# When columns that come back from DRAM are split, and how a memory's layer norm is laid out, in a two-layer hybrid decoder

## The chip, the core and the metric

The kernel runs on one core of one Trainium2 chip. A core has a matrix engine (PE; its weight loads are shown apart as PEld), a vector engine (DVE), a scalar engine (ACT), GpSimd (POOL) and a sync engine (SP). Each takes its own queue of instructions strictly in order, and they wait for each other by semaphores. SP and POOL also issue DMAs here, SP the loads of weights and constants, POOL the round trips through DRAM. Matrix products land in PSUM, which has eight banks per partition; all else lives in SBUF, 128 partitions wide.

The metric is the device time of one execution in microseconds. Lower is better. The median of three executions is the time of a version.

## What is computed

Two layers of a decoder over 256 positions with 1024 features, in float32. Each layer is a half-step SwiGLU block with its layer norm, three token mixers beside each other (a gated delta rule, a sliding-window attention, a cross-attention to a memory of 256 rows), a merge, a norm, and a second half-step SwiGLU block with its norm. Only these parts matter here:

```python
def swiglu(x, w_gu, w_down):
    gate, up = jnp.split(x @ w_gu, 2, axis=-1)       # D_FF = 2816
    return (jax.nn.silu(gate) * up) @ w_down

mem_n = layer_norm(mem, mem_ln_g, mem_ln_b)          # once, for both layers
for l in range(DEPTH):                               # DEPTH = 2
    x = layer_norm(ALPHA * x + 0.5 * swiglu(x, ffn1_gu[l], ffn1_down[l]), ...)
    ...
    k, v = jnp.split(mem_n @ w_mem_kv[l], 2, axis=-1)
    ...
    x = layer_norm(ALPHA * x + 0.5 * swiglu(x, ffn2_gu[l], ffn2_down[l]), ...)
```

`layer_norm` takes mean and variance over the 1024 features of a row, subtracts, multiplies by `rsqrt(var + 1e-5)`, scales by `g` and adds `b`.

## The kernel before

**Products in three passes.** Every float32 operand is split into a high part in a reduced format and the remainder (`split`, lines 115 to 117: a cast on ACT, then a subtraction on DVE), and a product is three matmuls: high by high, high by low, low by high (`mm3`). Weights come as one stream in the order of use, in units of 128 x 1024 words, 512 KB each. `unit` loads a unit on SP into `raw` (three buffers) and splits it into `whi` and `wlo` (five buffers each). So each unit costs ACT one cast and DVE one subtraction.

**The feed-forward block** (class `Ffn`, four times in the program). The 2816 hidden columns are worked in eleven groups of 256. For a group, PE computes gate and up for both halves of the positions, four units and 48 matmuls, into two PSUM banks of the pool `acc`, which has four. So two groups are in flight. `out` (lines 332 to 348) then does, for each half `tb`, a SiLU on ACT from PSUM to the tile `t` (line 338) and the product by `up` on DVE (line 339), which is the last reader of the half's bank. It follows a 32x32 block transpose on DVE (line 341), four stores on POOL to a DRAM tile `tr` (line 345) and one load on POOL back to SBUF (line 346), so that the hidden columns lie on partitions. The result is split again into a tile `u` (line 348): `u<-t` on ACT, `u<-t,u` on DVE. All of `t`, its transpose and the loaded columns share the tag `t2` with four buffers. After the eleven groups, `projA` multiplies the 22 `u` tiles by the down weights, 22 units, into banks for four outputs (`full_rows`: four banks of `acc` and one of `at`).

**What sets the order.** A planner lays out each engine's queue. It goes by priorities: what is traced earlier goes first among what it takes as ready; a unit's load and split are given a place 300 instructions earlier than where they are traced. Two marks bind it: `load` keeps a DMA on SP behind everything that was traced on SP before, and `issue_after(ins)` queues what a block traces on the engine of `ins`, and only on that engine, behind `ins`. The order is fixed when the program is built; on the chip an engine that waits for one instruction waits with all that stand behind it.

**The memory.** During the first feed-forward block of layer 0, `rest` calls small pieces of other work after given groups (the table `mid`; key `f` belongs to group `f // 2`). `memory_T` (lines 407 to 430) gives them: after f = 11 the two vectors `g` and `b` are loaded as broadcast rows of 512 KB each (`gb`), after 13 and 15 one half of the memory rows each is loaded into a tile `pp`, normed with `layernorm` (with the rsqrt done by integer start and three Newton steps, line 277) and turned by eight PE transposes into a PSUM tile `sm`, which is split into the tiles `mT` (`w0` to `w3`). After 16, `keep` stores these four tiles to DRAM, and layer 1 loads them again (`again`). `memory_kv` uses them right after the block.

Of the kernel before, what the change touches and what calls it, by code (L numbers as in the profile page):

```python
# [17 lines left out]
P = 128  # L18
# [19 lines left out]
@with_exitstack  # L38
def tile_trunk(ctx, tc, x, xT, mem, wst, lnp, memln, cvw, rows, cst, out):
    nc = tc.nc  # L40
# [55 lines left out]

    pos = [0]

    def unit(w=U, dst=None, cuts=1, behind=None):
        ahead = tc.high_priority(offset=AHEAD) if pos[0] >= 8 * P * U else nullcontext()  # L100
        raw = T(praw, [P, U], "raw")
        src = wst[pos[0]:pos[0] + P * w].rearrange("(p w) -> p w", p=P)
        pos[0] += P * w
        (ph, th), (pl, tl) = dst or ((phi, "whi"), (plo, "wlo"))
        with ahead:
            hi = T(ph, [P, U], th, F32R)
            lo = T(pl, [P, U], tl, F32R)
            for i in range(cuts):
                c = slice(i * w // cuts, (i + 1) * w // cuts)
                nc.sync.dma_start(raw[:, c], src[:, c])  # L110
                with tc.issue_after(behind) if behind else nullcontext():
                    split(hi[:, c], lo[:, c], raw[:, c])
        return hi, lo
# [58 lines left out]

    def projA(xt, w, kpu, nk, outs, tail=0, dsts=(), lead=0, after=None, behind=None, held=(), led=None):

# [26 lines left out]
        for uu in range(lead, nu - tail):  # L201
            for tb in range(2):
                run([uu], tb, range(len(outs[tb])))
        for uu in range(nu - tail, nu):
            get(uu)
# [47 lines left out]
    def layernorm(y, gB, bB, eps, src=None, fin=None, sizes=(512, 512)):  # L253
        n = min(sizes)
        st = T(p3, [P, 4, 6], "bnst")[:, :D // n, :]
        done = at_ = 0
        for j, size in enumerate(sizes):
            if src:
                src(j, slice(at_, at_ + size))
            at_ += size  # L260
            while done < at_:
                nc.vector.bn_stats(st[:, done // n, :], y[:, done:done + n])  # L262
                done += n
        mv = T(p3, [P, 2], "bnmv")
        nc.vector.bn_aggr(mv, st)  # L265
        rs = T(p3, [P, 1], "rstd")
        rt = T(p3, [P, 1], "rst")

        if src:
            nc.scalar.activation(rs, mv[:, 1:2], AF.Sqrt, bias=epsc[:, eps:eps + 1])  # L270
            nc.vector.reciprocal(rs, rs)
            nc.vector.scalar_tensor_tensor(rt, mv[:, 1:2], epsc[:, eps:eps + 1], rs, op0=ALU.add, op1=ALU.mult)
            nc.vector.scalar_tensor_tensor(rt, rt, -0.5, rs, op0=ALU.mult, op1=ALU.mult)
            nc.vector.scalar_tensor_tensor(rs, rt, 1.5, rs, op0=ALU.add, op1=ALU.mult)  # L274
        else:
            nc.vector.tensor_scalar(mv[:, 1:2], mv[:, 1:2], LN_EPS, None, ALU.add)
            rsqrt(rs, mv[:, 1:2], rt)
        for c in range(2):
            cc = slice(c * 512, (c + 1) * 512)
            nc.vector.scalar_tensor_tensor(y[:, cc], y[:, cc], mv[:, 0:1], gB[:, cc], op0=ALU.subtract, op1=ALU.mult)  # L280
            ins = nc.vector.scalar_tensor_tensor(y[:, cc], y[:, cc], rs, bB[:, cc], op0=ALU.mult, op1=ALU.add)  # L281
            if fin:
                fin(c)
        return ins.ins
# [9 lines left out]
    class Ffn:  # L294
        def __init__(self, before=None):
            self.units = []
            for q in range(KD // 2):
                if before:
                    before(q)
                self.units.append(unit(cuts=2 if before and q == 0 else 1))  # L300
            self.hu, self.bank = {}, {}

# [29 lines left out]
        def out(self, i, banks):  # L332
# [3 lines left out]
            for tb in range(2):  # L336
                g, u = (banks[tb][:, c:c + S].rearrange("p (j x) -> p j x", j=8) for c in (0, S))
                nc.scalar.activation(t[:, :, tb, :], g, AF.Silu)  # L338
                nc.vector.tensor_tensor(t[:, :, tb, :], t[:, :, tb, :], u, op=ALU.mult)  # L339
            z = T(p2, [P, 512], "t2", bufs=4)  # L340
# [5 lines left out]
            nc.gpsimd.dma_start(y, d.rearrange("b c q x -> (b c) (q x)"))  # L346
            hi, lo = (self.h(i)[:, n].rearrange("p a (t q s) -> p (a t) q s", t=2, q=4) for n in range(2))
            split(hi, lo, y.rearrange("p (q n s) -> p n q s", q=4, n=4))

        def rest(self, hT, tail, dsts, post, mid={}, behind=None):  # L350
            for i in range(1, NFT // 2):
# [9 lines left out]
                for f in (2 * i, 2 * i + 1):  # L361
                    if f in mid:
                        mid[f]()
            outs = full_rows()
            projA((lambda k: self.hu[k // 2][:, 0, k % 2, :], lambda k: self.hu[k // 2][:, 1, k % 2, :]), D, 1, NFT, outs, tail, dsts, after=post)

# [40 lines left out]
    def memory_T(mT, l):  # L407
# [13 lines left out]
        def vecs():  # L421
            got["gb"] = gb(memln[0], memln[1])
            mT.extend(T(pu, [P, 4, S], f"w{i}", F32R) for i in range(4))

        def rows_(tb):
            m = T(p2, [P, D], "pp")
            load(m, mem[tb * P:(tb + 1) * P, :])
            layernorm(m, *got["gb"], 0, None, lambda q: to_T(lambda q: (mT[q], mT[2 + q]), tb, m, q))

        return {13: again} if l else {11: vecs, 13: lambda: rows_(0), 15: lambda: rows_(1), 16: keep}  # L430

# [672 lines left out]
```

## Time and profile before

| | |
|---|---|
| median of 3 executions | 1369.0 us (1361.87 to 1371.48) |
| the profiled execution's own time | 1370.57 us |
| its span, first to last instruction | 1368.8 us |
| mean granted clock of PE | 0.977 of full speed |
| DMA, mean over the span | 192 GB/s |
| longest kinds of wait on ACT and DVE for the columns | ACT `u` for the load of `t` from `tr`: 130.9 us in 38 waits; DVE `u` for ACT `u`: 112.7 us in 45 |

A row of the profile's groups reads: line, engine, operation, what it writes `<-` what it reads, shapes, count | busy us in all, mean ns of one | idle us of the engine just before them, and what ended most of it. A row of the timeline starts with its time and its duration in us, and has in brackets how long the engine was idle before it and what it waited for. A row of stretches has the stretch, its length, the busy time of PE, PEld, DVE, ACT and POOL with the number of instructions, the granted clock of PE (1.00 is full), the DMA engines' busy share and GB/s. A row of waits has the total in us, the number and the longest.

### The profile page before, as it was taken

To read this page: it belongs to the slowest core of one execution; us is meant where nothing else is said; L and a number is where in the kernel's file an instruction comes from. 1 tells how busy PE (TensorE), PEld (TensorE's weight loads), DVE (VectorE), ACT (ScalarE), POOL (GpSimd) and SP (SyncE) were. 2 spreads that over 40 slices of the span, in tenths; PEclk is the share of its full clock that TensorE was granted. 3 is DMA by queue.
4 is the path that set the end of the run, shared out by engine and by line. 5 is a ranking of instruction groups with operands and counts; after the bars stand their busy time and mean duration, and the time that the engine had idled before them with its cause. 6 is when DMAs were issued, how large, how long until landed. Compare 5 with 4: busy or idle time off the path is not lost. (4 is left out here: it accounts for less than half of the span.)

```text
span 1368.8 us, 19252 instructions
## 1 busy us (share of the span) xinstructions
PE 1290.0 (94%) x7176; PEld 1099.4 (80%) x7176; DVE 850.7 (62%) x1270; ACT 652.6 (48%) x973; POOL 197.1 (14%) x355
## 2 busy tenths in 40 slices
PE   8979899999999999978999978999999999999797
PEld 6857789999878788766888757899987787887586
DVE  5576457796647865553675554668867388555445
ACT  6544343666665443443354343446657554444341
POOL 0222100002310012220011220000033100122200
PEclk9999999999999999998999998999999999999899
DMA  8878674755535647665677666656554355666663
GB/s 267 288 234 269 192 225 137 216 170 139 165 108 163 222 151 233 205 203 180 228 232 229 211 200 189 215 152 205 169 156 139 93 187 183 210 214 208 201 185 120
DMA packets 77726, 263.26 MB, mean 192 GB/s; under 512 B 11680, under 2 KB 12832, under 8 KB 77632
## 3 DMA queue, kind: packets, MB, share of 16 engines
q1 hardware_dynamic: 66176, 232.53, 52.9%
q0 software_dynamic: 11456, 29.51, 7.8%
q8 instruction: 56, 0.92, 0.3%
q14 instruction: 38, 0.31, 0.1%
HBM read 247.18 MB, written 14.81 MB: 191 GB/s over the span
## 5 line engine op out<-in xcount | busy, mean ns | idle before, releaser
L117 DVE TENSOR_TENSOR wlo<-raw,whi 128x1024 fp32r<-128x1024 f32 (+2 forms) x403 | 479.7, 1205 | 326.6 <-ACT whi L116 324.9
L116 ACT CAST whi<-raw 128x1024 fp32r<-128x1024 f32 (+2 forms) x403 | 410.0, 1034 | 441.4 <-DMA raw<-in_wst_dram 219.7
L126 PE MATMUL acc<-whi,hT 128*128 128x512 f32 (+1 forms) x1824 | 571.2, 389 | 25.1 <-DVE t L339 20.3
L126 PEld LDWEIGHTS acc<-whi,hT 128*128 128x128 f32 x1824 | 342.9, 189 | 99.9 <-DVE t L339 26.6
L126 PE MATMUL acc<-wlo,hT 128*128 128x512 f32 (+1 forms) x912 | 352.5, 387 | 0.3 <-DVE wlo L117 0.3
L126 PE MATMUL acc<-whi,u 128*128 128x512 f32 (+1 forms) x800 | 257.5, 386 | 30.8 <-DVE t L339 30.8
L126 PEld LDWEIGHTS acc<-whi,u 128*128 128x128 f32 x800 | 156.1, 197 | 63.0 <-DVE t L339 35.4
L126 PEld LDWEIGHTS acc<-wlo,hT 128*128 128x128 f32 x912 | 172.8, 189 | 33.2 <-DVE wlo L117 1.2
L345 POOL DMA_DIRECT2D tr<-t x176 | 96.1, 553 | 414.6 <-DVE t L341 407.7
L126 PE MATMUL acc<-wlo,u 128*128 128x512 f32 (+1 forms) x400 | 153.1, 383 | 0.0
L126 PE MATMUL acc<-hT,whi 128*128 128x256 f32 x672 | 122.3, 284 | 0.0
L126 PEld LDWEIGHTS acc<-hT,whi 128*128 128x128 f32 x672 | 104.7, 192 | 0.0
L117 DVE TENSOR_TENSOR u<-t,u 128x512 fp32r<-128x512 f32 x44 | 30.4, 691 | 104.6 <-ACT u L116 104.5
L126 PE MATMUL acc<-hT,wlo 128*128 128x256 f32 x336 | 95.0, 283 | 0.0
L116 ACT CAST u<-t 128x512 fp32r<-128x512 f32 x44 | 27.2, 619 | 130.9 <-DMA t<-tr 130.9
L126 PEld LDWEIGHTS acc<-wlo,u 128*128 128x128 f32 x400 | 78.8, 197 | 13.0
L126 PEld LDWEIGHTS acc<-hT,wlo 128*128 128x128 f32 x336 | 64.4, 192 | 0.0
L346 POOL DMA_DIRECT2D t<-tr x44 | 25.0, 568 | 184.9 <-DMA tr<-t 139.6
L126 PE MATMUL at<-whi,u 128*128 128x256 f32 x152 | 41.0, 294 | 0.0
L339 DVE TENSOR_TENSOR t<-t,acc 128x256 f32<-128x256 f32 x88 | 35.9, 414 | 3.5 <-ACT t L338 3.3
L473 DVE SCALAR_TENSOR_TENSOR t<-acc,cw,t 128x255 f32<-128x255 f32 (+2 forms) x72 | 34.4, 478 | 0.9
L338 ACT ACTIVATE t<-acc 128x256 f32<-128x256 f32 x88 | 32.6, 378 | 3.0 <-PE acc L126 3.0
(244 smaller groups left out, 1267.7 us busy)
## 6 DMA issues: line engine op xcount, KB each, us to landing
raw<-in_wst_dram SPq DMA_DIRECT2D x409, 512.0 KB, 4.3
tr<-t POOLq DMA_DIRECT2D x176, 64.0 KB, 3.7
t<-tr POOLq DMA_DIRECT2D x44, 256.0 KB, 3.2
raw<-in_wst_dram SPq DMA_DIRECT2D x16, 324.0 KB, 3.1
gB<-in_lnp_dram SPq DMA_DIRECT2D x6, 512.0 KB, 6.6
bB<-in_lnp_dram SPq DMA_DIRECT2D x6, 512.0 KB, 6.2
mdr<-w POOLq DMA_DIRECT2D x4, 512.0 KB, 6.0
w<-dr POOLq DMA_DIRECT2D x4, 512.0 KB, 10.4
```

The lines of the kernel that those rows point to most:

```text
L116: nc.scalar.copy(hi, src)
L117: return nc.vector.tensor_tensor(lo, src, hi.bitcast(F32), op=ALU.subtract).ins
L126: return pe(nc.tensor.matmul(*a, **k))
L338: nc.scalar.activation(t[:, :, tb, :], g, AF.Silu)
L339: nc.vector.tensor_tensor(t[:, :, tb, :], t[:, :, tb, :], u, op=ALU.mult)
L345: nc.gpsimd.dma_start(d[:, :, q].rearrange("b c x -> c b x"), z[32 * q:32 * q + 32].rearrange("c (b x) -> c b x", b=4))
L346: nc.gpsimd.dma_start(y, d.rearrange("b c q x -> (b c) (q x)"))
L473: nc.vector.scalar_tensor_tensor(yc[:, j, d:], b[:, j, :S - d], w[:, t:t + 1], yc[:, j, d:], op0=ALU.mult, op1=ALU.add)
```

## The change

Two things are changed. The split of the columns that come back from DRAM moves from the end of `out` to a new `settle`. It is called in the next group's `out`, behind the products of line 339, and for the last group in `projA`, behind the ninth unit of the down weights. The DVE half is queued behind the instruction given; the ACT half is only traced later. The small pieces of `mid` are queued, on DVE, behind the group's last product.

The memory's norm no longer turns rows into columns on PE. The host gives a second, feature-major copy of the memory (`memT`), and `mem_ln_g`, `mem_ln_b` by partitions. The row-major copy is read for the statistics only. Mean and reciprocal deviation of the 256 rows go through DRAM (512 words out, a broadcast of 2 KB to all 128 partitions back), and each half of the feature-major copy has the mean subtracted and the factor multiplied on DVE, is scaled and shifted on ACT with four instructions of 256 columns, and is split. The steps now stand at f = 8 (loads), 10 (statistics), 13 (load of the halves), 15, 17 (the halves) and 19 (`keep`).

```diff
@@ -94,7 +94,7 @@
         nc.scalar.copy(t.rearrange("p v k -> p (v k)"), zero.to_broadcast([P, 2 * S]))
 
 
-    pos = [0]
+    pos, newest = [0], [None]
 
     def unit(w=U, dst=None, cuts=1, behind=None):
         ahead = tc.high_priority(offset=AHEAD) if pos[0] >= 8 * P * U else nullcontext()
@@ -109,7 +109,7 @@
                 c = slice(i * w // cuts, (i + 1) * w // cuts)
                 nc.sync.dma_start(raw[:, c], src[:, c])
                 with tc.issue_after(behind) if behind else nullcontext():
-                    split(hi[:, c], lo[:, c], raw[:, c])
+                    newest[0] = split(hi[:, c], lo[:, c], raw[:, c])
         return hi, lo
 
     def split(hi, lo, src):
@@ -170,7 +170,7 @@
             (b,) = yield from projB_parts(xt, 2, 4)
             use(i, b)
 
-    def projA(xt, w, kpu, nk, outs, tail=0, dsts=(), lead=0, after=None, behind=None, held=(), led=None):
+    def projA(xt, w, kpu, nk, outs, tail=0, dsts=(), lead=0, after=None, behind=None, held=(), led=None, along=None):
 
         def one(k, kk, hi, lo, tb, j):
             ts = slice(tb * P, (tb + 1) * P)
@@ -201,6 +201,8 @@
         for uu in range(lead, nu - tail):
             for tb in range(2):
                 run([uu], tb, range(len(outs[tb])))
+            if along and uu == 8:
+                along(newest[0])
         for uu in range(nu - tail, nu):
             get(uu)
         turns = ()
@@ -266,15 +268,11 @@
         rs = T(p3, [P, 1], "rstd")
         rt = T(p3, [P, 1], "rst")
 
-        if src:
-            nc.scalar.activation(rs, mv[:, 1:2], AF.Sqrt, bias=epsc[:, eps:eps + 1])
-            nc.vector.reciprocal(rs, rs)
-            nc.vector.scalar_tensor_tensor(rt, mv[:, 1:2], epsc[:, eps:eps + 1], rs, op0=ALU.add, op1=ALU.mult)
-            nc.vector.scalar_tensor_tensor(rt, rt, -0.5, rs, op0=ALU.mult, op1=ALU.mult)
-            nc.vector.scalar_tensor_tensor(rs, rt, 1.5, rs, op0=ALU.add, op1=ALU.mult)
-        else:
-            nc.vector.tensor_scalar(mv[:, 1:2], mv[:, 1:2], LN_EPS, None, ALU.add)
-            rsqrt(rs, mv[:, 1:2], rt)
+        nc.scalar.activation(rs, mv[:, 1:2], AF.Sqrt, bias=epsc[:, eps:eps + 1])
+        nc.vector.reciprocal(rs, rs)
+        nc.vector.scalar_tensor_tensor(rt, mv[:, 1:2], epsc[:, eps:eps + 1], rs, op0=ALU.add, op1=ALU.mult)
+        nc.vector.scalar_tensor_tensor(rt, rt, -0.5, rs, op0=ALU.mult, op1=ALU.mult)
+        nc.vector.scalar_tensor_tensor(rs, rt, 1.5, rs, op0=ALU.add, op1=ALU.mult)
         for c in range(2):
             cc = slice(c * 512, (c + 1) * 512)
             nc.vector.scalar_tensor_tensor(y[:, cc], y[:, cc], mv[:, 0:1], gB[:, cc], op0=ALU.subtract, op1=ALU.mult)
@@ -298,7 +296,7 @@
                 if before:
                     before(q)
                 self.units.append(unit(cuts=2 if before and q == 0 else 1))
-            self.hu, self.bank = {}, {}
+            self.hu, self.bank, self.due = {}, {}, None
 
         def h(self, i):
             if i not in self.hu:
@@ -336,7 +334,8 @@
             for tb in range(2):
                 g, u = (banks[tb][:, c:c + S].rearrange("p (j x) -> p j x", j=8) for c in (0, S))
                 nc.scalar.activation(t[:, :, tb, :], g, AF.Silu)
-                nc.vector.tensor_tensor(t[:, :, tb, :], t[:, :, tb, :], u, op=ALU.mult)
+                ins = nc.vector.tensor_tensor(t[:, :, tb, :], t[:, :, tb, :], u, op=ALU.mult).ins
+            self.settle(ins)
             z = T(p2, [P, 512], "t2", bufs=4)
             nc.vector.transpose(z, t.rearrange("p j t x -> p (j t x)"))
             y = T(p2, [P, 512], "t2", bufs=4)
@@ -344,8 +343,16 @@
             for q in range(4):
                 nc.gpsimd.dma_start(d[:, :, q].rearrange("b c x -> c b x"), z[32 * q:32 * q + 32].rearrange("c (b x) -> c b x", b=4))
             nc.gpsimd.dma_start(y, d.rearrange("b c q x -> (b c) (q x)"))
-            hi, lo = (self.h(i)[:, n].rearrange("p a (t q s) -> p (a t) q s", t=2, q=4) for n in range(2))
-            split(hi, lo, y.rearrange("p (q n s) -> p n q s", q=4, n=4))
+            self.due = (i, y)
+
+        def settle(self, behind):
+
+            if self.due:
+                (i, y), self.due = self.due, None
+                hi, lo = (self.h(i)[:, n].rearrange("p a (t q s) -> p (a t) q s", t=2, q=4) for n in range(2))
+                with tc.issue_after(behind):
+                    split(hi, lo, y.rearrange("p (q n s) -> p n q s", q=4, n=4))
+            self.last = behind
 
         def rest(self, hT, tail, dsts, post, mid={}, behind=None):
             for i in range(1, NFT // 2):
@@ -360,9 +367,10 @@
                 self.out(i, banks)
                 for f in (2 * i, 2 * i + 1):
                     if f in mid:
-                        mid[f]()
+                        with tc.issue_after(self.last):
+                            mid[f]()
             outs = full_rows()
-            projA((lambda k: self.hu[k // 2][:, 0, k % 2, :], lambda k: self.hu[k // 2][:, 1, k % 2, :]), D, 1, NFT, outs, tail, dsts, after=post)
+            projA((lambda k: self.hu[k // 2][:, 0, k % 2, :], lambda k: self.hu[k // 2][:, 1, k % 2, :]), D, 1, NFT, outs, tail, dsts, after=post, along=self.settle)
 
     class Post:
 
@@ -419,15 +427,46 @@
                 nc.gpsimd.dma_start(mdr[i], flat(t.bitcast(F32)))
 
         def vecs():
-            got["gb"] = gb(memln[0], memln[1])
+            got["st"] = T(pu, [P, 2, 2], "mst")
+            got["gb"] = T(pu, [P, 2, KD], "mgb")
+            load(got["gb"], memln)
             mT.extend(T(pu, [P, 4, S], f"w{i}", F32R) for i in range(4))
-
-        def rows_(tb):
-            m = T(p2, [P, D], "pp")
-            load(m, mem[tb * P:(tb + 1) * P, :])
-            layernorm(m, *got["gb"], 0, None, lambda q: to_T(lambda q: (mT[q], mT[2 + q]), tb, m, q))
-
-        return {13: again} if l else {11: vecs, 13: lambda: rows_(0), 15: lambda: rows_(1), 16: keep}
+            got["m"] = [T(p2, [P, D], "pp") for _ in range(2)]
+            for tb in range(2):
+                load(got["m"][tb], mem[tb * P:(tb + 1) * P, :])
+
+        def rows_():
+
+            for tb in range(2):
+                mv = T(p3, [P, 2], "bnmv")
+                st = T(p3, [P, 4, 6], "bnst")[:, :2, :]
+                for j in range(2):
+                    nc.vector.bn_stats(st[:, j, :], got["m"][tb][:, j * 512:j * 512 + 512])
+                nc.vector.bn_aggr(mv, st)
+                nc.vector.tensor_copy(got["st"][:, 0, tb:tb + 1], mv[:, 0:1])
+                nc.vector.tensor_scalar(mv[:, 1:2], mv[:, 1:2], LN_EPS, None, ALU.add)
+                rsqrt(got["st"][:, 1, tb:tb + 1], mv[:, 1:2], T(p3, [P, 1], "rst"))
+            d = T(pd, [2, 2, P], "ms")
+            nc.gpsimd.dma_start(d.rearrange("a t p -> p a t"), got["st"])
+            got["row"] = T(pu, [P, D], "gB")[:, 0:512]
+            nc.gpsimd.dma_start(got["row"], d.rearrange("a t p -> (a t p)").partition_broadcast(P))
+
+        def halves_():
+            got["m"] = [T(p2, [P, 4, S], "pp") for _ in range(2)]
+            for q in range(2):
+                load(got["m"][q], memT_[:, q])
+
+        def half(q):
+            m = got["m"][q]
+            mean, rs = (got["row"][:, c:c + S].unsqueeze(1).to_broadcast([P, 4, S]) for c in (0, S))
+            nc.vector.tensor_tensor(m, m, mean, op=ALU.subtract)
+            nc.vector.tensor_tensor(m, m, rs, op=ALU.mult)
+            for j in range(4):
+                g, b = (got["gb"][:, n, 4 * q + j:4 * q + j + 1] for n in range(2))
+                nc.scalar.activation(m[:, j], m[:, j], AF.Identity, bias=b, scale=g)
+            split(mT[q], mT[2 + q], m)
+
+        return {13: again} if l else {8: vecs, 10: rows_, 13: halves_, 15: lambda: half(0), 17: lambda: half(1), 19: keep}
 
     def memory_kv(mT, behind):
         mx = (lambda k: mT[k // 4][:, k % 4, :], lambda k: mT[2 + k // 4][:, k % 4, :])
@@ -1083,9 +1122,10 @@
         "x": i["x"][0],
         "xT": np.ascontiguousarray(i["x"][0].T),
         "mem": i["mem"][0],
+        "memT": np.ascontiguousarray(i["mem"][0].T.reshape(2, 4, P, S).transpose(2, 0, 1, 3)),
         "wst": _stream(i),
         "lnp": np.stack([i["ln_g"], i["ln_b"]], 2),
-        "memln": np.stack([i["mem_ln_g"], i["mem_ln_b"]]),
+        "memln": np.ascontiguousarray(np.stack([i["mem_ln_g"], i["mem_ln_b"]]).reshape(2, KD, P).transpose(2, 0, 1)),
         "cvw": np.ascontiguousarray(i["dn_conv_w"].reshape(NL, 4, 12, P).transpose(3, 0, 2, 1)),
         "rows": np.concatenate([i["swa_sinks"], i["dn_a_log"], i["dn_dt_bias"], i["dn_norm_w"]], 1),
         "cst": _consts(),
```

More of the change, by code (lines that the diff above doesn't have):

```diff
@@ L38, in tile_trunk @@
 @with_exitstack
-def tile_trunk(ctx, tc, x, xT, mem, wst, lnp, memln, cvw, rows, cst, out):
+def tile_trunk(ctx, tc, x, xT, mem, memT_, wst, lnp, memln, cvw, rows, cst, out):
     nc = tc.nc
```

## The prediction, made before the changed kernel ran

> **What bounds the kernel now.** I read the page first, then the table of waits of PE, then the timelines of ACT, DVE, POOL and PE through one period of the second feed-forward block of layer 0, and last tables of busy time over chosen stretches.
>
> ```profile
> span 1368.8 us, 19252 instructions
> PE 1290.0 (94%) x7176; PEld 1099.4 (80%) x7176; DVE 850.7 (62%) x1270; ACT 652.6 (48%) x973; POOL 197.1 (14%) x355
> L126 PE MATMUL acc<-whi,hT 128*128 128x512 f32 (+1 forms) x1824 | 571.2, 389 | 25.1 <-DVE t L339 20.3 <-ACT whi L116 4.8
> L126 PE MATMUL acc<-whi,u 128*128 128x512 f32 (+1 forms) x800 | 257.5, 386 | 30.8 <-DVE t L339 30.8
> L116 ACT CAST u<-t 128x512 fp32r<-128x512 f32 x44 | 27.2, 619 | 130.9 <-DMA t<-tr 130.9
> ...
> PE acc L126 <- DVE t L339: 51.1, 24, 6.2
> ...
> L129 PE MATMUL sm<-cs,pp 128*128 128x128 f32 x16 | 3.6, 387 | 9.7 <-DVE pp L281 7.9 <-issue 1.8
> ```
>
> PE is busy for 94% of the span, so what can be won is its idle time, 1368.8 - 1290.0 = 78.8 us, and whatever part of its busy time runs slowly. Of the idle time 51.1 us (24 waits) end with the product of line 339, which frees a PSUM bank: 20.3 us where a group of the gate/up product starts, 30.8 us where the four down projections start. Another 9.7 us lie ahead of the 16 transposes of the memory's norm (last row). Why is line 339 late, though it takes 0.41 us? The timelines say:
>
> ```profile
> 598.33 0.50 PE L126 MATMUL acc<-whi,hT 128*128 128x512 f32 x1 [1.15 <-DVE t L339]
> ...
> 587.92 0.37 ACT L338 ACTIVATE t<-acc 128x256 f32<-128x256 f32 x1
> 592.00 1.05 ACT L116 CAST whi<-raw 128x1024 fp32r<-128x1024 f32 x1 [3.71 <-DMA raw<-in_wst_dram]
> 596.60 0.62 ACT L116 CAST u<-t 128x512 fp32r<-128x512 f32 x1 [3.54 <-DMA t<-tr]
> 597.13 0.38 ACT L338 ACTIVATE t<-acc 128x256 f32<-128x256 f32 x1
> ...
> 608.95 0.62 ACT L116 CAST u<-t 128x512 fp32r<-128x512 f32 x1 [3.44 <-DMA t<-tr]
> 609.47 0.38 ACT L338 ACTIVATE t<-acc 128x256 f32<-128x256 f32 x1
> ...
> 597.25 0.69 DVE L117 TENSOR_TENSOR u<-t,u 128x512 fp32r<-128x512 f32 x1 [2.94 <-ACT u L116]
> 597.86 0.41 DVE L339 TENSOR_TENSOR t<-t,acc 128x256 f32<-128x256 f32 x1
> 598.31 0.71 DVE L341 STREAM_TRANSPOSE t<-t 128x512 f32<-128x512 f32 x1
> 609.60 0.69 DVE L117 TENSOR_TENSOR u<-t,u 128x512 fp32r<-128x512 f32 x1 [2.83 <-ACT u L116]
> 610.21 0.41 DVE L339 TENSOR_TENSOR t<-t,acc 128x256 f32<-128x256 f32 x1
> ...
> 599.32 2.17 POOL L345 DMA_DIRECT2D tr<-t  x4 [5.08 <-DVE t L341]
> ...
> 30.00:73.00 43.00, 43.00 (x191) 35.60 (x190) 24.46 (x29) 21.71 (x28) 8.80 (x16) 1.00 0.87 289
> ```
>
> The trip is a loop. ACT takes its queue in order, and the cast of the columns back from DRAM (`u<-t`, 596.60) stands between the two SiLUs of the next group (587.92 and 597.13). Only the second SiLU lets line 339, the 32x32 transpose (598.31), the four stores and the load go, and that load ends at 608.95, where the next cast has been waiting 3.44 us, again with a SiLU behind it. So the loop takes 609.47 - 597.13 = 12.34 us a group, of which 608.95 - 598.31 = 10.64 us are the trip. PE needs 48 matmuls at 43.00 / 191 = 0.225 us (last row, from layer 0's first block: PE is full there), 10.8 us. The loop loses 1.5 us a group; four PSUM banks hide the first half of each block, and the rest shows as PE's idle time.
>
> **The change, part by part.**
>
> *The split behind the next group's product.* No instruction is added. The pair (ACT cast, DVE difference) is traced after the next group's SiLUs and products, and the DVE half is pinned behind the second product. The ACT half is pinned to nothing: its place is the planner's choice. Today the cast was traced earlier than these SiLUs, so of two that are ready it goes first. In the rows it follows a weight cast that follows the first SiLU. The two banks' last matmuls lie 3 x 0.225 = 0.7 us apart and a weight cast takes 1.05 us, so after that cast the second SiLU is ready too, and only the order of tracing decided. The change turns it over. I take it that the SiLU goes first. Early groups already have both SiLUs ahead of the cast, and PE does not wait there:
>
> ```profile
> 506.18 0.65 ACT L338 ACTIVATE t<-acc 128x256 f32<-128x256 f32 x2
> 509.83 0.62 ACT L116 CAST u<-t 128x512 fp32r<-128x512 f32 x1 [0.84 <-DMA t<-tr]
> ...
> 506.00:517.00 11.00, 11.00 (x50) 9.12 (x49) 8.05 (x10) 5.85 (x9) 2.17 (x4) 1.00 0.78 250
> ```
>
> What stays is this. (a) The start of a down projection: the last group's second bank is free after a weight cast 0.95, SiLU 0.38, a weight difference 1.2 and the product 0.41 = 2.9 us, against 9 matmuls, 2.0 us, that need not wait: 0.9 us x 4 = 3.6 us. (b) The wait does not vanish: behind the cast now stand the weight casts, and behind the DVE half (609.60) the transpose, if the planner puts it there. Then transposes follow each other at 10.64 + 0.65 (cast to difference) + 0.61 (difference to the next) = 11.9 us, 1.1 us over the product. PE does not feel that at once: the banks are freed ahead of it, and ACT and DVE have a group and a quarter of weights cast ahead (five buffers, 13.6 us at 4 units a group). From some 3 us at the first group the lag grows to 3 + 10 x 1.1 = 14 us at the last, so only the last two groups lose 1 to 3 us each. In layer 0's first block the trips are longer (the cast of 63.72 waits 5.00, below), so the lag passes 13.6 us earlier. Bounds 0 (transpose first) to 19 us (3 x 3 + 10); I take the middle, 9.
>
> ```profile
> 63.72 0.62 ACT L116 CAST u<-t 128x512 fp32r<-128x512 f32 x1 [5.00 <-DMA t<-tr]
> ```
>
> Line 339: 51.1 - 3.6 - 9 = 38.5 us gained.
>
> *What the long gaps cost afterwards.* Behind each long gap PE runs at half rate:
>
> ```profile
> 152.50:158.40 5.90, 5.88 (x18) 5.06 (x19) 2.71 (x3) 2.09 (x2) 2.75 (x5) 0.50 0.47 109
> ...
> 1301.80:1305.30 3.50, 3.44 (x12) 3.05 (x13) 1.95 (x3) 1.04 (x1) 2.17 (x4) 0.51 0.32 67
> sum 35.00, PE 34.72 PEld 28.32 DVE 17.25 ACT 11.69 POOL 13.13; mean PE 4.34 PEld 3.54 DVE 2.16 ACT 1.46 POOL 1.64
> ...
> 791.40:800.00 8.60, 8.60 (x38) 7.09 (x39) 5.54 (x6) 3.26 (x5) 2.74 (x5) 1.00 0.72 217
> 791.32 0.50 PE L126 MATMUL acc<-whi,hT 128*128 128x512 f32 x1 [3.24 <-DVE t L339]
> 1294.37 0.50 PE L126 MATMUL acc<-whi,u 128*128 128x512 f32 x1 [3.35 <-DVE t L339]
> ```
>
> Eight stretches of the feed-forward blocks, 35.0 us at a granted clock of 0.50, lose half: 17.4 us. A gap of 3.24 us left the clock at 1.00, one of 3.35 us halved it. With gaps of about 1 us left, all of it should go; a few long gaps may stay, so 15 (bounds 0 and 17.4). The Trainium skill ("TensorE: Matmul & The Clock Gate", What's actually happening) lets the clock fall after an idle window of about 3.4 us that runs free; by that rule a gap under 3.4 us costs only itself most of the time, and the sum here would be 17.4 in place of 15. The trace agrees, at 3.24 against 3.35 us.
>
> *The memory's norm.* It leaves PE:
>
> ```profile
> 109.47 0.63 PE L129 MATMUL sm<-cs,pp 128*128 128x128 f32 x4 [1.79 <-issue]
> 93.30:96.90 3.60, 3.60 (x13) 3.21 (x14) 3.56 (x7) 1.33 (x2) 0.57 (x1) 0.50 0.71 198
> sum 7.00, PE 7.00 PEld 6.04 DVE 6.70 ACT 3.19 POOL 1.65; mean PE 3.50 PEld 3.02 DVE 3.35 ACT 1.60 POOL 0.83
> ...
> L117 DVE TENSOR_TENSOR wlo<-raw,whi 128x1024 fp32r<-128x1024 f32 x15 | 18.1, 1211 | 3.4 <-ACT whi L116 3.4
> L262 DVE BATCH_NORM_STATS2 bnst<-pp 128x6 f32<-128x512 f32 x4 | 2.6, 683 | 0.0
> L280 DVE SCALAR_TENSOR_TENSOR pp<-pp,bnmv,gB 128x512 f32<-128x512 f32 x4 | 2.9, 741 | 0.0
> L281 DVE SCALAR_TENSOR_TENSOR pp<-pp,rstd,bB 128x512 f32<-128x512 f32 x4 | 2.9, 749 | 0.0
> L117 DVE TENSOR_TENSOR w<-sm,w 128x512 fp32r<-128x512 f32 x4 | 2.7, 674 | 0.0
> ...
> w<-dr POOLq DMA_DIRECT2D x4, 512.0 KB, 10.4
> ```
>
> Gone from PE: 9.7 us idle, half of 7.0 us that ran at 0.50 behind it (3.5), and 16 transposes at 0.63 / 4 = 0.16 us (2.5): 15.7 us. DVE: 2.9 + 2.9 + 2.7 us go; four subtractions and products and two differences of 1024 columns come, 6 x 1.21 = 7.3 us, and two small copies: about equal. ACT: four casts of 512 columns go (2.5 us by the 0.62 of `u<-t`), eight scale-and-shift passes of 256 columns at the SiLU's 0.38 us and two casts at 1.05 come: 2.6 us more, on an engine that is busy for 48% of the span. SP: two broadcast loads of 512 KB go, two halves of 512 KB and 8 KB come: even. POOL gets a store of 512 words and its broadcast, 256 KB; no row has elements that small, so the two together cost POOL between nothing and the longest landing on its queue (10.4 us, last row). The new waits, and what stands behind them: POOL's store waits for DVE's statistics (2.6 us of sums and some two dozen one-column steps, traced behind the sixth group's product), its broadcast for that store, and behind both stand the next group's stores, so one trip of the loop may be up to 10 us late, which the lead partly absorbs: 0 to 8 us, I take 4, nearer to the usual landing. SP's loads of the halves wait until the statistics have read the two `pp` buffers, with weight loads behind them; they come a group, 10.8 us, after the statistics, which covers it. DVE's first half waits for the broadcast, two groups, 21.6 us, after its cause: covered; without that cover it would hold the weight differences by up to 10 us. The store of the finished copy (`keep`) moves behind the tenth group: the same four DMAs on POOL. Gained: 11.7 us.
>
> *Sum.* 38.5 + 15 + 11.7 = 65 us against the profiled execution's own 1370.57 us: 1305; that execution is 1.6 us over the median of the runs, so 1304. All gains whole (51.1 - 3.6 + 17.4 + 15.7 = 80.6) give 1290; that is the low end, with 2 us for the runs' spread.
>
> **The rivals.**
>
> *The cast stays ahead of the second SiLU* (the change does not do what it says). It is pinned to nothing on ACT, and if the planner takes the columns as landed before the weight cast, it stays. For it: nothing in the rows shows the planner's slack. Against it: today it stands behind the weight cast in every such period. Only the DVE difference leaves the loop, 597.86 - 597.25 = 0.61, less the wait for the SiLU, 0.38 us a wait: 24 x 0.4 = 9 us, with the memory's 11.7: 1350, or 1346 if the gaps of 3.35 us fall below 3.24 and keep the clock.
>
> *The wait moves to DVE and reaches PE.* If the lead is worth less than 13.6 us, the loop of 11.9 us binds PE: the 20.3 us shrink to 20.3 x 1.1 / 1.5 = 15, the 30.8 us to some 12, and 6 of the 17.4 us stay: 1370.6 - 24 - 11.4 - 11.7 = 1323.
>
> *Slower.* The planner puts the cast ahead of both SiLUs. Then trip 10.64, cast 0.5, SiLU 0.4, weight cast 1.0, SiLU and product 0.8 and the difference 0.6 follow each other: 13.9 us, 3.1 over the product; it eats the lead in three groups and shows in some eight a block: 32 x 3.1 = 99 us against today's 51, 1370 + 48 - 12 = 1406. It decides if the columns pass as landed 0.7 us before the last matmul; today's order (cast behind the weight cast) speaks against it.
>
> **How the numbers follow.** Forecast 0.66 (1288 to 1325 by itself), the wait on DVE 0.13, cast kept 0.13, slower 0.08. The range 1288 to 1350 leaves out the slower case, half of the kept cast and a little below. About 1% (13.7 us) can be told from no change: forecast, DVE and 0.6 of the kept cast are faster, 0.87; the rest of it is the same, 0.05; slower 0.08.
>
> **What would show it.** Right: both SiLUs ahead of `u<-t` on ACT in every group; PE's wait for line 339 under 16 us; no stretch at 0.50 inside the blocks; no PE transposes from `pp`. Wrong: SiLUs still right behind `u<-t`, at 12 us a group; new PE waits for `whi` or `wlo` late in a block; POOL's stores late in the groups behind the statistics.

## The result and the profile after

| | before | after |
|---|---|---|
| median of 20 runs each | 1368.17 us (1361.87 to 1374.19) | 1358.12 us (1354.36 to 1363.26) |
| profiled span | 1368.8 us | 1355.4 us |
| mean granted clock of PE | 0.977 | 0.980 |

The ratio is 0.9925, with a 95% interval of 0.991 to 0.994: a gain of about 10 us, where 64 were forecast (1304 us). First the head of the page of the changed kernel, then three of its groups, then PE's table of waits (total, number, longest, in us).

```profile
span 1355.4 us, 19229 instructions
PE 1294.4 (96%) x7160; PEld 1097.7 (81%) x7160; DVE 845.7 (62%) x1266; ACT 654.6 (48%) x979; POOL 197.8 (15%) x357
```

```profile
L126 PE MATMUL acc<-whi,hT 128*128 128x512 f32 (+1 forms) x1824 | 572.0, 391 | 15.1 <-ACT whi L116 15.1
...
L126 PE MATMUL acc<-wlo,hT 128*128 128x512 f32 (+1 forms) x912 | 355.9, 390 | 8.9 <-DVE wlo L117 8.9
...
L126 PE MATMUL acc<-whi,u 128*128 128x512 f32 (+1 forms) x800 | 257.6, 386 | 24.0 <-DVE t L337 24.0
```

```profile
PE acc L126 <- DVE t L337: 24.0, 9, 6.4
PE acc L126 <- ACT whi L116: 15.1, 8, 4.9
PE acc L126 <- DVE wlo L117: 8.9, 11, 1.0
```

The product that frees the banks (line 339 before, 337 now) makes PE wait 24.0 us instead of 51.1, and where a gate/up group starts no longer at all. But PE now waits for weights: 15.1 us for `whi` (4.9 of it the start of the program, 4.8 before) and 8.9 for `wlo`. PE's idle time, 1355.4 - 1294.4 = 61.0 us, is 17.8 us less than before; its busy time grew by 4.4 us, so the span fell by 13.4. Why the weights are late stands in the timelines of ACT, DVE and PE, at the same block as in the prediction:

```profile
588.26 0.62 ACT L116 CAST u<-t 128x512 fp32r<-128x512 f32 x1 [5.35 <-DMA t<-tr]
588.79 2.93 ACT L116 CAST whi<-raw 128x1024 fp32r<-128x1024 f32 x3
591.63 0.37 ACT L336 ACTIVATE t<-acc 128x256 f32<-128x256 f32 x1
595.54 1.05 ACT L116 CAST whi<-raw 128x1024 fp32r<-128x1024 f32 x1 [3.54 <-PE acc L126]
596.50 0.38 ACT L336 ACTIVATE t<-acc 128x256 f32<-128x256 f32 x1
600.43 0.62 ACT L116 CAST u<-t 128x512 fp32r<-128x512 f32 x1 [3.56 <-DMA t<-tr]
```

```profile
499.08 0.71 DVE L340 STREAM_TRANSPOSE t<-t 128x512 f32<-128x512 f32 x1
...
597.77 0.41 DVE L337 TENSOR_TENSOR t<-t,acc 128x256 f32<-128x256 f32 x1
601.09 0.69 DVE L117 TENSOR_TENSOR u<-t,u 128x512 fp32r<-128x512 f32 x1 [2.90 <-ACT u L116]
601.70 0.70 DVE L340 STREAM_TRANSPOSE t<-t 128x512 f32<-128x512 f32 x1
...
628.16 0.70 DVE L340 STREAM_TRANSPOSE t<-t 128x512 f32<-128x512 f32 x1
```

```profile
589.88 0.49 PE L126 MATMUL acc<-whi,hT 128*128 128x512 f32 x1 [1.57 <-ACT whi L116]
591.39 0.79 PE L126 MATMUL acc<-wlo,hT 128*128 128x512 f32 x1 [1.01 <-DVE wlo L117]
```

Both SiLUs (591.63 and 596.50) now stand ahead of the cast, as forecast. But the second product is done at 598.18, and the transpose that only needs it starts at 601.70: on DVE the difference `u<-t,u` stands between them, and it waits for the cast, which waits for the previous trip. The loop through DRAM is closed again, by way of DVE. From the block's first transpose to its eleventh it takes (628.16 - 499.08) / 10 = 12.91 us a group, against PE's 10.8; in the other three blocks it is 13.15, 12.13 and 12.47 us. Each time ACT stands at its cast (5.35 us here), the next weight casts stand behind it, and PE runs out of `whi` (1.57) and then of `wlo` (1.01).

The second new thing is in the memory's block. The timelines of POOL and of ACT:

```profile
97.22 0.77 POOL L450 DMA_DIRECT2D ms<-mst  x1 [3.27 <-DVE mst L253]
101.04 1.10 POOL L344 DMA_DIRECT2D tr<-t  x2 [3.06 <-DVE t L340]
106.96 0.56 POOL L452 DMA_DIRECT2D gB<-ms  x1 [4.81 <-DMA ms<-mst]
107.51 1.10 POOL L344 DMA_DIRECT2D tr<-t  x2
```

```profile
98.78 0.62 ACT L116 CAST u<-t 128x512 fp32r<-128x512 f32 x1 [5.24 <-DMA t<-tr]
...
109.40 1.05 ACT L116 CAST whi<-raw 128x1024 fp32r<-128x1024 f32 x1 [6.87 <-DMA raw<-in_wst_dram]
...
116.70 0.62 ACT L116 CAST u<-t 128x512 fp32r<-128x512 f32 x1 [5.97 <-DMA t<-tr]
```

The broadcast of the statistics stands between the second and the third of a group's four stores and waits for the store of the statistics, so this trip is late: 116.70 - 98.78 = 17.9 us from cast to cast. And until 106.96, while that 2 KB store is under way, the weights are late too (6.87).

### The profile page after: what moved, and what is told of

Same layout as the page of the kernel before. It is cut to its first block, busy times and chain, and to the rows that moved or that the text cites. A ratio compares the mean times of both kernels' runs of the same rounds, so it can differ in the third digit from the quotient of the medians.

```text
span 1355.4 us, 19229 instructions
## 1 busy us (share of the span) xinstructions
PE 1294.4 (96%) x7160; PEld 1097.7 (81%) x7160; DVE 845.7 (62%) x1266; ACT 654.6 (48%) x979; POOL 197.8 (15%) x357
## 4 chain that ended last, share of the span: by engine, by line
PE 50%; DMA 27%; DVE 8%; issue 6%; ACT 6%; POOL 3%; SPq 0%; POOLq 0%; DVEq 0%; ACTq 0%
PE acc L126 40%; DMA t<-tr 9%; DMA raw<-in_wst_dram 9%; DMA tr<-t 9%; PE at L126 4%; DVE wlo L117 3%; POOL tr L344 3%; ACT whi L116 3%; PE sm L126 3%; ACT u L116 2%; DVE t L340 2%; PE sm L129 1%; DMA ms<-mst 1%; DVE u L117 1%; PE at L129 0%
## 5 line engine op out<-in xcount | busy, mean ns | idle before, releaser
L126 PE MATMUL acc<-whi,hT 128*128 128x512 f32 (+1 forms) x1824 | 572.0, 391 | 15.1 <-ACT whi L116 15.1
L126 PE MATMUL acc<-whi,w 128*128 128x512 f32 (+1 forms) x96 | 31.0, 392 | 2.7 <-DVE w L117 2.7
```

The lines of the kernel that those rows point to most:

```text
L126: return pe(nc.tensor.matmul(*a, **k))
```

## The experiments

Each version was run six times. Its ratio is to the kernel before, measured beside it (median 1367.25 us beside `e1` to `e4`, 1366.25 beside `e5` to `e8`, 1367.83 beside `e9` to `e12`).

| version | median, us | ratio, 95% interval |
|---|---|---|
| `e1_turn_first` | 1309.0 | 0.957 (0.954 to 0.959) |
| `e2_split_only` | 1340.3 | 0.980 (0.977 to 0.984) |
| `e3_memory_only` | 1381.5 | 1.011 (1.007 to 1.014) |
| `e4_broadcast_sp` | 1351.8 | 0.988 (0.984 to 0.991) |
| `e5_wide_store` | 1303.8 | 0.955 (0.952 to 0.957) |
| `e6_pe_rows` | 1304.7 | 0.955 (0.952 to 0.958) |
| `e7_turn_rows` | 1302.3 | 0.953 (0.950 to 0.956) |
| `e8_after_wide` | 1349.0 | 0.987 (0.984 to 0.990) |
| `e9_rows_late_keep` | 1299.5 | 0.951 (0.948 to 0.954) |
| `e10_late_rows` | 1299.6 | 0.951 (0.948 to 0.953) |
| `e11_after_wide_late` | 1346.1 | 0.984 (0.981 to 0.987) |
| `e12_words_alone` | 1300.5 | 0.951 (0.948 to 0.954) |

The length of each feed-forward block, worked out from PE's timeline of each profiled run, from the start of its unbroken run of gate/up matmuls to the end of the unbroken run of its down projection, in us (L0 and L1 are the layers):

| | first, L0 | second, L0 | first, L1 | second, L1 |
|---|---|---|---|---|
| before | 197.1 | 181.7 | 185.4 | 182.5 |
| after | 198.3 | 176.8 | 177.9 | 176.2 |
| `e2` split only | 191.4 | 173.2 | 177.6 | 174.7 |
| `e3` memory only | 203.1 | 185.6 | 183.4 | 186.9 |
| `e1` turn first | 191.9 | 160.8 | 165.6 | 166.1 |
| `e4` broadcast on SP | 200.7 | 172.9 | 177.7 | 176.5 |
| `e8` after, wide store | 196.1 | 168.3 | 181.8 | 180.1 |
| `e11` after, wide store, late keep | 191.5 | 172.6 | 180.1 | 176.0 |
| `e5` turn first, wide store | 189.9 | 160.5 | 165.1 | 163.9 |
| `e7` turn first, norm by rows | 186.1 | 160.2 | 165.4 | 164.7 |
| `e9` turn first, PE rows, late keep | 182.4 | 161.0 | 165.5 | 163.4 |

One warning for reading it: in `after`, `e4`, `e8` and `e11` every engine has the same order of work in the second block, and yet that block takes 168.3 to 176.8 us. While the loop binds, a difference of a few us in one block of one trace shows nothing by itself.

**Is it the order on DVE?** One line moves:

```diff
-            self.settle(ins)
             z = T(p2, [P, 512], "t2", bufs=4)
-            nc.vector.transpose(z, t.rearrange("p j t x -> p (j t x)"))
+            self.settle(nc.vector.transpose(z, t.rearrange("p j t x -> p (j t x)")).ins)
```

> The changed kernel with one thing moved: the split of the returned columns is queued on DVE behind the 32x32 transpose of the next group (line 340) instead of behind its second product (line 337), so that the transpose no longer stands behind a difference that waits for the round trip. Theory A (the loop of the round trip is unbroken in the changed kernel, it only runs through the DVE difference now, 12.8 us a group): the transposes follow the products at PE's 10.8 us, most of the 24.0 us of waits for line 337 and of the 24.0 us of new waits for whi and wlo go, 1358 - 35 to 45 = 1313 to 1323 us. Theory B (the weight casts behind the waiting ACT cast, or the supply of weights, bind by themselves, whatever the transpose waits for): within 5 us of the changed kernel, 1353 to 1363 us.

1309.0 us: theory A, and by more than it asked. DVE's timeline and PE's waits in this version:

```profile
492.64 0.71 DVE L339 STREAM_TRANSPOSE t<-t 128x512 f32<-128x512 f32 x1
...
567.15 0.42 DVE L337 TENSOR_TENSOR t<-t,acc 128x256 f32<-128x256 f32 x1
567.60 0.71 DVE L339 STREAM_TRANSPOSE t<-t 128x512 f32<-128x512 f32 x1
570.37 0.69 DVE L117 TENSOR_TENSOR u<-t,u 128x512 fp32r<-128x512 f32 x1 [2.06 <-ACT u L116]
...
600.44 0.71 DVE L339 STREAM_TRANSPOSE t<-t 128x512 f32<-128x512 f32 x1
```

```profile
PE acc L126 <- DVE t L337: 10.8, 4, 5.4
PE acc L126 <- ACT whi L116: 9.0, 3, 5.0
PE acc L126 <- DVE wlo L117: 2.0, 3, 0.8
```

The transpose follows its product at once, and the ten intervals of the same block are (600.44 - 492.64) / 10 = 10.78 us, PE's own pace (12.50, 10.79 and 11.18 us in the other three blocks). The difference still waits (2.06), but nobody needs it soon. That rules out theory B.

**Which part of the change gave and which took?** `e2` is the deferred split with the memory's norm by rows; `e3` is the memory's new norm with the split at the end of `out` as before. The telling lines of the two edits:

```diff
...
-        return {13: again} if l else {8: vecs, 10: rows_, 13: halves_, 15: lambda: half(0), 17: lambda: half(1), 19: keep}
+        return {13: again} if l else {11: vecs, 13: lambda: rows_(0), 15: lambda: rows_(1), 16: keep}
```

> The deferred split alone, with the memory's norm as it was before (rows, PE transposes). Theory C (the memory's part gives nothing: what leaves PE comes back as late stores on POOL in the same block): 1358 us, within 3 of the changed kernel. Theory D (the memory's part holds the 11.7 us that were predicted for it, and the deferred split gives nothing or loses): 1368 to 1372 us.

```diff
...
-            self.due = (i, y)
+            hi, lo = (self.h(i)[:, n].rearrange("p a (t q s) -> p (a t) q s", t=2, q=4) for n in range(2))
+            split(hi, lo, y.rearrange("p (q n s) -> p n q s", q=4, n=4))
```

> The memory's norm on the feature-major copy alone, with the split of the returned columns at the end of each group as before. Theory C (the memory's part gives nothing): 1366 to 1370 us, like the kernel before. Theory D (it holds its 11.7 us): 1355 to 1359 us.

Neither theory held: the split alone gives 1367.25 - 1340.3 = 27 us, and the memory's part does not gain nothing, it loses: 14.3 us by itself (1381.5 against 1367.25), 17.8 us beside the split (1358.1 against 1340.3). In the table of blocks 6.0 and 6.9 us of that lie in the block where the memory's work stands (203.1 - 197.1, 198.3 - 191.4). The other 8 and 11 us lie behind it, where the order of work is the same with and without the change of the norm; no experiment explains them.

**Does it lose only through the loop?** `e7` is `e1` with the norm by rows, the edits of `e1` and `e2` together.

> The transpose ahead of the split, with the memory's norm as it was before (rows, 16 PE transposes). Theory G (the memory's part is worth the predicted 11.7 us once the loop no longer binds, and cost time in the changed kernel only through the loop): 1316 to 1322 us. Theory H (it costs in its own block, by late weights and late stores, whether the loop binds or not): 1297 to 1305 us.

1302.3: theory H. With the loop open the memory's part still costs 6.7 us, 5.8 of it in its block (191.9 - 186.1).

**Is it the broadcast on POOL?**

```diff
-            got["row"] = T(pu, [P, D], "gB")[:, 0:512]
-            nc.gpsimd.dma_start(got["row"], d.rearrange("a t p -> (a t p)").partition_broadcast(P))
+            got["d"] = d
...
                 load(got["m"][q], memT_[:, q])
+            got["row"] = T(pu, [P, D], "gB")[:, 0:512]
+            load(got["row"], got["d"].rearrange("a t p -> (a t p)").partition_broadcast(P))
```

> The changed kernel with the broadcast of the memory's statistics taken off POOL: SP loads it, three sixths of a block later, with the halves of the memory (f = 13); the store of the statistics stays on POOL. If the broadcast between a group's four stores makes the trip of 17.9 us and with it PE's gap of 3.77 + 1.01 us at 118 to 120 us: the trip falls to about 12 us, the gap goes, 1352 to 1356 us. If the gap has another cause, or is paid later in the same block by the loop: 1357 to 1360 us.

1351.8 is the time of the first case, but the trace does not show its cause: the first block did not get shorter (200.7 us against 198.3), and the store still took 9.3 us to land. Most of the gain lies in the second block, where nothing was changed and trips were shorter in that run. Inconclusive.

**Is it the single words?** The store of the statistics writes 512 words to 512 places. `e5` (on `e1`) and `e8` (on the changed kernel) turn them first:

```diff
...
-            nc.gpsimd.dma_start(d.rearrange("a t p -> p a t"), got["st"])
+            z = T(pu, [P, 32], "msz")
+            nc.vector.transpose(z, got["w"])
+            for b in range(4):
+                nc.gpsimd.dma_start(d.rearrange("a t p -> (a t) p")[:, 32 * b:32 * b + 32], z[32 * b:32 * b + 4])
```

> The kernel with the transpose ahead of the split (1309.0 us) with one more thing: the memory's statistics are turned by a 32x32 transpose on DVE first, so that the 2 KB go to DRAM as 16 rows of 128 bytes in four stores instead of 512 single words in one. Theory E (the single words clog the DMA engines: while that store was under way, the engines were busy for 88% of 98 to 102 us and moved 37 GB/s, and the next weights landed in 10.4 us instead of 4.4): no load of raw over 7 us there, PE's gap of 3.85 us at 109 us is gone, 1303 to 1306 us. Theory F (the gap comes from the load of the memory's halves and from POOL's order, whatever the size of the words): 1308 to 1311 us, the two added stores included.

> The changed kernel with the wide store of the statistics (16 rows of 128 bytes in four stores) and nothing else. Theory E: the gaps of 3.77 and 1.01 us at 118 to 120 us shrink and the trip of 16 us there falls to 12, 1350 to 1355 us. Theory F: 1357 to 1360 us.

1303.8 (5.1 less) and 1349.0 (9.1 less): both times are those of theory E. The DMA view between 94 and 112 us (KB each, median us from issue to landing), first of `e1`, then of `e5`:

```profile
raw<-in_wst_dram SPq DMA_DIRECT2D x4, 512.0 KB, 10.7
...
ms<-mst POOLq DMA_DIRECT2D x1, 2.0 KB, 10.0
```

```profile
raw<-in_wst_dram SPq DMA_DIRECT2D x4, 512.0 KB, 4.3
...
ms<-msz POOLq DMA_DIRECT2D x4, 0.5 KB, 3.8
```

The weights are no longer late there, though one gap of PE only moved (`e5` has one of 3.10 us at 113 us). For `e8` the size stays open: its first block is 2.2 us shorter than that of the changed kernel, the trip (transpose to cast) fell from 16.6 to 14.8 us and not to 12, the edit also moved other instructions of that block in the queues, and its second block is 8.5 us shorter with nothing changed in it. To see the words by themselves, `e12` adds one store of 512 words of a constant tile to `e7`; it is not read, and every other instruction keeps its place.

> The transpose ahead of the split with the memory's norm in rows (1302.3 us), with one DMA more and nothing else changed in any engine's order: 512 single words of a constant tile are stored to DRAM on POOL, behind the load of the sixth group, and nobody reads them. Theory E (single words hold up all DMA engines for some 10 us): loads of raw beside it land in 8 us or more, 1305 to 1309 us. Theory F (a 2 KB store costs its issue, 0.78 us on POOL, and no more): 1301 to 1304 us.

The DMA view between 88 and 104 us (KB each, median us from issue to landing), and PE's next wait, first of `e7`, then of `e12`:

```profile
raw<-in_wst_dram SPq DMA_DIRECT2D x5, 512.0 KB, 4.0
...
tr<-t POOLq DMA_DIRECT2D x4, 64.0 KB, 2.4
```

```profile
104.28 1.12 PE L129 MATMUL sm<-cs,pp 128*128 128x128 f32 x4 [6.31 <-DVE pp L283]
```

```profile
raw<-in_wst_dram SPq DMA_DIRECT2D x4, 512.0 KB, 7.4
...
tr<-t POOLq DMA_DIRECT2D x4, 64.0 KB, 8.9
ms<-cs POOLq DMA_DIRECT2D x1, 2.0 KB, 9.2
```

```profile
109.06 1.12 PE L129 MATMUL sm<-cs,pp 128*128 128x128 f32 x4 [11.09 <-DVE pp L283]
```

```profile
94.00:98.00 4.00, 3.97 (x18) 2.96 (x16) 2.96 (x4) 2.52 (x3) 2.15 (x4) 1.00 0.52 35
```

The effect is plain: beside the words a load of weights lands in 7.4 us instead of 4.0 and a store of columns in 8.9 instead of 2.4. The last row, a stretch of `e12`, has the DMA engines busy for 52% at 35 GB/s. PE waits 4.8 us longer (POOL was 1.4 us behind already when it issued the words) and the block ends 4.1 us later (195.2 against 191.1 us). The whole time does not show it: 1300.5 against 1302.3, each over a range of six us, below both theories' ranges. In the two traces 3.6 us are still there where the last block's first transpose starts (1124.3 against 1120.7 us); then PE waits 2.30 and 1.73 us at that block's down projection in `e7` and not in `e12`. So the words' price in place is shown, and their share of the total only by `e5`.

**Without DRAM at all.** In `e6` four matmuls put the rows on all partitions, in place of the store and the broadcast:

```diff
...
+            ps = sm()
+            for c in range(4):
+                a, t = c // 2, c % 2
+                matmul(ps[:, c * P:(c + 1) * P], got["st"][:, a, t:t + 1].to_broadcast([P, P]), ident, start=True, stop=True)
+            got["row"] = T(pu, [P, D], "gB")[:, 0:512]
+            nc.scalar.copy(got["row"], ps)
```

> The kernel with the transpose ahead of the split (1309.0 us), with the statistics' round trip through DRAM taken out: four matmuls of 128 columns, the statistic's column as broadcast weights against the identity, lay the four rows on all partitions in one PSUM bank, and ACT copies them. Theory E: the gap of 3.85 us and the store's and the broadcast's 17 us on POOL's queue go, for four matmuls of 0.16 us and one copy: 1300 to 1305 us, at or below the version with the wide store. Theory F: 1307 to 1311 us.

1304.7: at the edge of theory E and no better than the wide store, because a new wait took the place of the old: PE reached the matmuls before the statistics were done (4.48 + 0.55 us). A gap at the start of the down projection was there too, here in PE's timeline:

```profile
143.63 0.77 PE L126 MATMUL acc<-whi,u 128*128 128x512 f32 x1 [5.21 <-DVE t L337]
```

**The store of the finished copy.** `e9` queues `keep`, 2 MB in four stores, behind the last group's load; `e10` also traces the four matmuls and the copy at f = 15; `e11` puts `keep` late in the changed kernel with the wide store.

```diff
+            self.loaded = nc.gpsimd.dma_start(y, d.rearrange("b c q x -> (b c) (q x)")).ins
...
+        keep = mid.pop(19, None)
...
+        if l == 0:
+            with tc.issue_after(f1.loaded):
+                keep()
         kv = memory_kv(mT, post.end)
```

The edit that `e10` adds, with the six lines of `e6` above moved as well:

```diff
         def half(q):
             m = got["m"][q]
+            if q == 0:
+                ps = sm()
...
+                nc.scalar.copy(got["row"], ps)
```

> The version with the statistics laid out by PE (1304.7 us), with keep's four stores of 512 KB queued on POOL behind the last group's load instead of among the last three groups. Theory K (those 2 MB, moved to the end of the block by the change, slow the weights and the last trip there: 0.89 of DMA busy at 135 to 145 us, PE's gap of 5.21 us at 143.6 us and half rate behind it): the gap falls below 2 us, 1296 to 1300 us. Theory L (the gap is the start of the down projection itself, as in the other blocks): 1303 to 1307 us.

> The version with PE rows and late stores of keep, with the four matmuls and the copy traced two sixths of a block later, at the first half (f = 15), so that PE does not reach them before the statistics are done. Today PE waits 4.48 + 0.55 us there. If nothing takes its place: 5 to 8 us (with the half rate) below the version with the late stores alone. If the halves on DVE, which then wait for the copy, hold the weight differences: no gain, or up to 5 us more.

> The changed kernel (split behind the second product, as in the change) with the wide store of the statistics and with keep's stores behind the last group's load. If these two are what the memory's part costs: from 1349.0 us (wide store alone) to 1338 to 1343 us, as the deferred split alone (1340.3). If the late stores don't matter: 1346 to 1351 us.

`e9`: 1299.5, theory K; the gap of 5.21 us is gone and the down projection of that block takes 50.8 us instead of 57.4. `e10`: 1299.6, no gain. PE no longer waits for the statistics and starts the down projection 5.6 us sooner, but there a weight cast that waits 3.00 us for its load stands ahead of the last SiLUs on ACT, and PE waits 5.17 us. `e11`: 1346.1, at the edge of the case in which the late stores don't matter, and 2.9 us under `e8`, with ranges that overlap. Its first block is now as long as that of `e2` (191.5 and 191.4 us), which fits with the words and `keep` being the memory's cost there, in one trace each. The 5.8 us to `e2` lie behind that block, where the queues of DVE, ACT and POOL have the same order in both; where they come from stays open.

The best versions, `e9` and `e10`, are 4.9% below the kernel before and 58.6 us below the change. The norm by rows (`e7`, 1297.5 to 1303.9 us) can't be told from them (`e9`, 1298.1 to 1303.6): even at its best, the new norm is not shown to gain anything.

## Why the prediction was wrong

*The bound, and the order on ACT: right.* The loop was the bound, the SiLUs moved ahead of the cast, and what the split could give was sized well: its gains whole were 51.1 - 3.6 + 17.4 = 64.9 us, and `e7`, where the loop is open, gains 1366.25 - 1302.3 = 64 us. That is no luck of the sum: in its trace PE's waits for the product fall from 51.1 to 6.5 us, and the only half-rate stretch left in which PE works is one of 6.8 us at the memory's transposes.

*The failed step is (b) of the first part.* The text saw that the transpose would stand behind the difference and costed that loop at 11.9 us, 1.1 over the product, hidden by a lead of 13.6 us: 9 us in all, the middle between 0 and 19. The term that was too small is the trip. It was taken from one group (10.64 us); from transpose to cast the mean of ten groups of the same block is 11.65 us in the trace of after, and 11.65 + 0.65 + 0.61 = 12.91 us is the measured loop, 2.1 over the product. The trace of before had 11.17 us there already. So the lag grows to some 3 + 21 = 24 us, not 14, and about 10 us a block are left over the lead; PE's waits in this block add to 9.8 us. In PE's waits over the program: 24.0 + 10.2 + 8.9 = 43.1 us are left of 51.1, where 12.6 were forecast. The choice of 9 failed too: by the text's own numbers 14 us of lag against a lead of 13.6 leave 0.4 us a block, not 1 to 3 us in each of two groups, and between ends as far apart as 0 and 19 the middle had no row behind it. The bound "0 (transpose first)" was the right order and was one line away. Alone, the split gave 27 us (`e2`) of the 53.5 forecast for it (38.5 + 15).

*The half rate: nothing came.* 15 us were forecast. The stretches in which PE worked at half clock add to 41.6 us of work before and 40.8 after, so the half rate cost 20.8 and 20.4 us; the 20.8 are what the prediction had read, 17.4 and 3.5. Long gaps stayed at the down projections, and pairs of short ones did harm that the text excluded (below). In `e7` it is 4.4 us of work, a cost of 2.2 us.

*The memory's norm: the wrong sign.* Forecast: 11.7 us gained. Measured: 14 to 18 us lost in the loop-bound kernels, 6.7 with the loop open. PE's waits for the transposes did go. The price of the new work was bounded by the landing of the store and the broadcast on POOL's own queue. Each landed within it (9.5 and 5.6 us in the trace of after; one behind the other they exceed it), and the trip between them came about 5 us late (17.9 against a mean loop of 13.15 in that block), near the 4 us taken. But the words also slowed the loads of weights, on another queue, and that was not on the list of what is queued behind what. The move of `keep` was costed at nothing, "the same four DMAs on POOL": at its new place it costs 5.2 us more than behind the block's last load (`e6` to `e9`). The rest of the loss stays open.

*The rivals.* "The wait moves to DVE and reaches PE" is what happened. Its 1323 us had the memory's 11.7 in it; without them it is 1335, and `e2`, which is that case, measured 1340.3. The cast did not stay ahead of the second SiLU, nor did it move ahead of both. Of the signs named for being right, the order on ACT and the missing PE transposes came; PE's wait for the product (24.0 us, not under 16) and the half-rate stretches did not go. Two of the signs for being wrong came: new waits for `whi` and `wlo`, and late stores on POOL behind the statistics.

## What to carry to other kernels

A wait moved along an in-order queue is only gone when nothing of the next round stands behind it on any engine: follow the loop through every queue it crosses, and put the instruction that feeds the next trip (here the transpose) ahead of the one that consumes the last. Size a loop by its mean over many rounds, first row to last, never by one round, and compare with the pace of the engine it feeds. A transfer's price isn't its bytes: count its pieces, and look at what lands beside it on other queues. And look at pairs of short gaps too, not only at the longest one.

## What the runs showed of the hardware that was not expected

*Single words.* A store of 2 KB as 512 words took 9.2 to 10.0 us to land, as 16 rows of 128 bytes 1.6 to 3.8 us (`e8`, `e5`), and loads of 512 KB on another queue took about twice as long meanwhile. The Trainium skill ("DMA: Bandwidth & Descriptors", Specifications) says that transfers under 512 bytes are done as read, modify and write; the traces show the slowness, not that mechanism, and 128 bytes, also under that size, were far cheaper than 4. The wide store also has 16 pieces in place of 512; no run tells the size of a piece from their number.

*Two short gaps halve the clock.* A stretch of the changed kernel behind the two waits at 589.88 and 591.39 above (clock in the column before the last two):

```profile
590.00:591.00 1.00, 0.37 (x1) 0.06 (x1) 1.00 (x2) 1.00 (x2) 0.48 (x1) 0.95 0.00 0
591.00:592.00 1.00, 0.61 (x2) 0.52 (x3) 1.00 (x2) 1.00 (x2) 1.00 (x3) 0.50 0.26 66
...
593.00:594.00 1.00, 1.00 (x4) 0.81 (x3) 0.94 (x2) 0.00 (x0) 0.00 (x0) 0.50 0.64 258
```

Gaps of 1.57 and 1.01 us with one matmul between them brought the granted clock to 0.50, while a single gap of 3.24 us in the kernel before left it at 1.00. In the same trace 0.63 and 1.01 us (at 787 us) halved it too, 0.35 and 1.01 us (at 553 us) did not. A gap of under 3.4 us does not cost only itself, as the prediction took from the Trainium skill ("TensorE: Matmul & The Clock Gate", What's actually happening); how little work PE did over some three us seems to matter, and no run here isolates it.
